# Two-layer decoder trunk on one core: four units of second-row products kept back ahead of an inner norm, and one more weight residual of the next stage issued early

## Chip, cores and metric

The kernel runs on 1 core of one Trainium2 chip. The metric is device time in microseconds (us); lower is better. The kernel before takes 2195.03 us, the median of 3 runs (2194.04 to 2196.49).

## What is computed

A trunk of two layers works on x, 256 rows (positions) of 2048 float32 values. Each layer has two sub-layers, a token mixer and a gated feed-forward with a short convolution, and each sub-layer ends in a LayerNorm:

```python
for i in range(DEPTH):                       # DEPTH = 2
    mod = c_act @ ada_w[i] + ada_b[i]        # 6 vectors of 2048 from the condition c
    sh1, sc1, g1, sh2, sc2, g2 = split(mod, 6)
    h = x * (1 + sc1) + sh1
    y = fox_attention(h, w_in, b_f, w_o) if i == 0 else swa_attention(h, pos, w_in, sinks, w_o)
    x = layer_norm(ALPHA * x + (1 + g1) * y, ln_mix_g[i], ln_mix_b[i])
    h = x * (1 + sc2) + sh2
    y = conv_ffn(h, w_up, conv_w, conv_b, w_down)
    x = layer_norm(ALPHA * x + (1 + g2) * y, ln_ffn_g[i], ln_ffn_b[i])
```

Everything is float32. A LayerNorm needs the mean and variance of a whole row of x, so all 2048 columns of a row have to be there before the next sub-layer's h can be formed from it. There are four norms: three inner ones, called A (after the mixer of layer 0, near 455 us), B (after the feed-forward of layer 0, near 1188 us) and C (after the mixer of layer 1, near 1451 us), and the last one at the end.

## The kernel before, in words

**Tiles.** The 256 rows are two halves of 128 (`NT` = 2): the first rows (t = 0) and the second rows (t = 1). TensorE multiplies in a reduced-precision format, so every operand is split into a high and a low part, and one product takes three matmuls: high by high, high by low, low by high. For weights the high part `wh` is a cast on ScalarE (line 254) and the low part, the residual `wl`, a subtraction on VectorE (line 265).

**Units.** `stream` (line 233) walks a block of 512 weight columns in units of 256 contraction rows. For each unit it issues a DMA (half of a 1 MB tile in pool `wp`, 6 buffers), the cast into `wh`, and puts a function `go` into the list `work`. `go` runs the unit's matmuls, steps the deferred generators (`run_post`), takes one of the `feeds`, and calls `tick`. The pool `hl` holds 4 pairs `wh`, `wl`. Three units are pending at a time (`settle(2)`).

**When a residual is issued.** `rest` (line 202) walks the work list from the item that is about to run and issues the residuals of the units that it meets until it has counted three units (two, if the item is no unit). Items put in with `then(fn, True)` are in the set `lone`: at the first of these the count is raised to two (lines 206 and 207). At a norm three lone items stand between the last unit of the stage and the first of the next: the deferred last `residual`, `flush`, and `between`. The units of the next stage are called u0', u1', u2', u3' here.

**The end of a stage.** The last column block (d = 3) before a norm uses `x_mm_end` (line 284) with n = 2 in the three inner norms: the last n units multiply for the first rows only; the second rows' products of these units are kept back and run together behind them. So the first rows' sums are complete some time before the second rows'. `residual` (line 534) then does for each half, on VectorE: `tmp = ps * gate` (line 537), `x += tmp` (539), `bn_stats` (544), `bn_aggr` (547), `+EPS` (549), and a power on GpSimd (550) that gives 1/sigma. For the first rows a further small operation, `nm` = -mu/sigma (line 543), is pinned behind the second rows' addition. The last norm of the kernel uses n = 8 with four units' pairs placed in the buffer `hpad` (`spares`, line 309).

**Between stages.** `between` (line 1068) lets TensorE do filler matmuls (`spin`), then `modulate` (485) runs two feeds ahead of the first unit: `normalise` (554; first rows on ScalarE, line 560, second rows on VectorE, line 562), transposes of x on TensorE (446), and the modulation into `hH` and `hL` (lines 456 to 458 for the first four blocks, 460, 464, 84 and 85 for the rest). The remaining six feeds go one per unit.

**What sets the order.** The instructions are traced in the order of the work list, and a list scheduler at build time may move an instruction ahead of earlier ones on its engine where it takes it to be ready sooner. `pin` puts an instruction behind the one traced just before it on its engine. `behind[0] = 2` (line 1077) pins the next two residuals after a norm.

**The condition vectors.** `mod` is computed on VectorE as a background task: 192 columns, each a 1 MB DMA into a `wp` buffer and one multiply-reduce (`wa`, line 364). `tick` adds `ada["rate"]` to a debt and runs one column when the debt reaches 1; after the scale vector of a sub-layer's second half the task is held until the next `between`.

Of the kernel before, what the change touches and what calls it, by code (L numbers as in the profile page):

```python
# [14 lines left out]
ALU = mybir.AluOpType  # L15
# [3 lines left out]
D = 2048  # L19
S = 256  # L20
NT = S // P
KC = D // P
# [14 lines left out]
WB = 512  # L37
# [4 lines left out]
def hybrid_trunk(ctx: ExitStack, tc: tile.TileContext, a: dict, out: bass.AP):  # L42
    nc = tc.nc
# [33 lines left out]
    def pin(ins, on=True):  # L77

        if on:
            tc.keep_in_program_order(ins)  # L80
# [47 lines left out]
    for j in range(D // WB):  # L128
        ps = bank("cb")
# [72 lines left out]
    def rest(*items):  # L202

        n = 0
        for f in items:
            if f in lone:
                n = max(n, 2)
            if f in residuals:
                residuals[f]()
                n += 1  # L210
            elif f in weights:
                n += 1
            if n > 2 - (items[0] not in weights):
                return
# [60 lines left out]
    def x_mm(ps, kc, h, l, stat, last, first=0, ts=range(NT), js=range(2)):  # L275

        for t in ts:
            for i in js:
                xh, xl = stat(kc + i, t)
                mm(ps[t], xh, h[:, i, :], start=kc + i == first)  # L280
                mm(ps[t], xh, l[:, i, :])
                mm(ps[t], xl, h[:, i, :], stop=kc + i == last)

    def x_mm_end(ps, stat, nk, n):

        kept = []

        def use(kc, h, l):
            end = kc >= nk - 2 * n
            x_mm(ps, kc, h, l, stat, nk - 1, ts=(0,) if end else range(NT))  # L290
            if end:
                kept.append((kc, h, l))
            if kc + 2 >= nk:
                for e in kept:
                    x_mm(ps, *e, stat, nk - 1, ts=(1,))

        return use
# [8 lines left out]
                mm(o, wh, hL[:, kc + i, :], skip_group_check=True)  # L306
                mm(o, wl, hH[:, kc + i, :], stop=kc + i == last, skip_group_check=True)

    def spares(nk):
        t = [hpad[:, 56 + i * 2 * WB:56 + (i + 1) * 2 * WB].rearrange("p (a f) -> p a f", a=2) for i in range(8)]  # L310
        return {nk - 16 + 2 * i: (t[2 * i], t[2 * i + 1]) for i in range(4)}

    def x_stationary(wsrc, col, k0, nk, stat, end=0):

        ps = x_banks()
        use = x_mm_end(ps, stat, nk, end) if end else lambda kc, h, l: x_mm(ps, kc, h, l, stat, nk - 1)
        stream(wsrc, k0, col, list(range(nk)), use, spares(nk) if end == 8 else {})
        return ps

    def w_stationary(wsrc, col):  # L320
# [213 lines left out]
    def residual(ps, d, gate, last):  # L534
        for t in range(NT):
            tmp = ttile()
            nc.vector.tensor_tensor(tmp, ps[t], gate[:, d * 512:(d + 1) * 512], op=ALU.mult)
            xs = x[:, t, d * 512:(d + 1) * 512]
            nc.vector.tensor_tensor(xs, xs, tmp, op=ALU.add)  # L539
            if last:  # L540
                if t == 1 and d == D // 512 - 1:
                    mu, rs, nm = moments[0]
                    pin(nc.vector.scalar_tensor_tensor(nm, mu, -1.0, rs, op0=ALU.mult, op1=ALU.mult))
                nc.vector.bn_stats(stats[:, t, d, :], xs)  # L544
                if d == D // 512 - 1:
                    mv = sp.tile([P, 2], F32, tag="mv", name="mv")
                    nc.vector.bn_aggr(mv, stats[:, t].rearrange("p a b -> p (a b)"))
                    rs = sp.tile([P, 2], F32, tag="rs", name="rs")
                    nc.vector.tensor_scalar_add(mv[:, 1:2], mv[:, 1:2], EPS)
                    nc.gpsimd.tensor_tensor(rs[:, 0:1], mv[:, 1:2], mhalf, op=ALU.pow)  # L550
                    moments[t] = (mv[:, 0:1], rs[:, 0:1], rs[:, 1:2])
            yield
# [101 lines left out]
    def out_proj(oT, full, w_o, l):  # L654
        def stat(kc, t):
            while kc not in full:
                step()
            return oT[kc][0][:, t * P:(t + 1) * P], oT[kc][1][:, t * P:(t + 1) * P]

        ps = {d: x_banks() for d in range(2)}  # L660

        def part(d, ks):
            use = x_mm_end(ps[d], stat, KC, 2) if d == D // WB - 1 else                 lambda kc, h, l_: x_mm(ps[d], kc, h, l_, stat, KC - 1)
            stream(w_o, 0, d * WB, ks, use)

        for i, ks in enumerate((range(0, 8), range(8, 12))):
            then(lambda i=i: ada.update(rate=(0.72, 0.43)[l]))
            for d in range(2):
                part(d, list(ks))
        then(lambda: (ada_need(l, 2), ada.update(rate=(0.72, 0.65)[l])))  # L670
        for d in range(D // WB):
            if d < 2:
                part(d, list(range(12, KC)))
            else:
                ps[d] = x_banks()
                part(d, list(range(KC)))
            then(lambda d=d: defer(residual(ps[d], d, gates[l, 2], True)), d == D // WB - 1)
        then(lambda: (flush(), ada.update(gate_free=True)), True)
# [320 lines left out]
    def conv_ffn(l):  # L999
        w_up, w_dn = a["ffn_w_up"][l], a["ffn_w_down"][l]  # L1000
        NB = DFF // WB
        cw = lambda j, f: ccol[:, l, j, f:f + 1]

        def conv(pf, f):
            u = tp.tile([P, S], F32, tag="u", bufs=3, name="u")
            nc.scalar.activation(u, pf, AF.Identity, bias=cw(CW, f), scale=cw(2, f))  # L1006
            nc.vector.scalar_tensor_tensor(u[:, 1:], pf[:, :S - 1], cw(1, f), u[:, 1:],  # L1007
                                           op0=ALU.mult, op1=ALU.add)
            nc.vector.scalar_tensor_tensor(u[:, 2:], pf[:, :S - 2], cw(0, f), u[:, 2:],  # L1009
                                           op0=ALU.mult, op1=ALU.add)  # L1010
            return u

        def evac(ps, f0, then):
            u = None
            for f in range(5):
                v = conv(ps[f // 2][:, f % 2, :], f0 + f) if f < 4 else None
                if u is not None:
                    then(f - 1, u)
                u = v
                yield  # L1020
                yield

# [12 lines left out]

        sbs = [(0, 6), (6, NB)]
        if l == 0:
            then(lambda: later([rotary()]))
        for si, (b0, b1) in enumerate(sbs):
            gT = []  # L1040
            then(lambda: ada.update(rate=(0.32, 0.2)[l]))
            for b in range(b0, b1):
                ps = w_stationary(w_up, b * WB)
                sil = [ttile("sil") for _ in range(2)]
                then(lambda ps=ps, b=b, sil=sil: defer(evac(ps, b * 4, silu(sil))))
                ps = w_stationary(w_up, DFF + b * WB)
                then(lambda ps=ps, b=b, sil=sil, gT=gT: defer(evac(ps, DFF // P + b * 4, gated(sil, gT))))

            def stat(kc, t, gT=gT):
                while kc >= len(gT):  # L1050
                    run_post()
                return gT[kc][:, 0, t * P:(t + 1) * P], gT[kc][:, 1, t * P:(t + 1) * P]

            def ready(si=si):
                if si == 0:
                    drain()
                ada_need(l, 5)
                ada["rate"] = (0.45, 0.2)[l]

            then(ready)  # L1060
            for d in range(D // WB):
                ps = x_stationary(w_dn, d * WB, b0 * 4, (b1 - b0) * 4, stat, (2, 8)[l] if si > 0 and d == D // WB - 1 else 0)
                then(lambda ps=ps, d=d, si=si: defer(residual(ps, d, gates[l, 5], si == len(sbs) - 1)),
                     si > 0 and d == D // WB - 1)
        then(lambda: (flush(), ada.update(gate_free=True)), True)


    def between(l, v, g, b, name, ll):

        ada_need(l, v)  # L1070
        ada_need(l, v + 1)
        place(60 if v else 32)
        o = bank("spin")
        ada["held"] = False
        spin(o, 3)
        modulate(*merged(l, v, g, b, ll), normalise, o)
        behind[0] = 2
        later([affine(name, ll, 0 if v else 7)])

    for l in range(DEPTH):  # L1080
# [60 lines left out]
```

## Time and profile before

| | before |
|---|---|
| median of 3 runs | 2195.03 us (2194.04 to 2196.49) |
| profiled execution, its own time | 2194.81 us |
| span in the profile | 2193.0 us |
| TensorE matmul (PE) busy | 2138.1 us, 97% |
| VectorE (DVE) busy | 1764.0 us, 80% |
| ScalarE (ACT) busy | 1161.5 us, 53% |
| bytes read from HBM | 594.18 MB, 272 GB/s over the span |
| granted TensorE clock, mean | 0.993 |

How to read what follows. A row of the timeline has the start and duration in us, the engine, the line of the kernel, the operation, the tile written and the tiles read, the count, and in brackets the idle time of the engine just before it with what ended it. A row of the windows view has the stretch, its length, and the busy time of each engine in it with the number of instructions, then the granted TensorE clock (1.00 is full speed), the DMA share and GB/s. PE is the matmul side of TensorE and PEld its weight loads; SPq is the queue that issues DMAs. A matmul's end is modelled, so starts are the better mark.

### The profile page before, as it was taken

Reading aid. Unit: us, or ns where it says so; the run is one execution under the profiler, and the core shown is the slowest. Engines: PE = TensorE matmul, PEld = TensorE weight load, DVE = VectorE, ACT = ScalarE, POOL = GpSimd, SP = SyncE. Lnnn points to the kernel's source line nnn. Section 1 sums busy time; section 2 is a strip of 40 time slices with the busy share of each in tenths; the row PEclk is TensorE's granted clock in tenths of the full one; section 3 lists DMA queues with packets and bytes.
Section 4 is the critical chain, followed back from the end, with each engine's and each line's share of the span. In section 5 each row is a group of like instructions: output and inputs, shape, how many; then the busy total and the mean of one; then the engine's idle time right before and its main releaser. Section 6 shows DMA issues by size and latency. Waiting matters only on the chain.

```text
span 2193.0 us, 36167 instructions
## 1 busy us (share of the span) xinstructions
PE 2138.1 (97%) x14694; PEld 1948.5 (89%) x14694; DVE 1764.0 (80%) x2412; ACT 1161.5 (53%) x1771; POOL 11.5 (1%) x34
## 2 busy tenths in 40 slices
PE   6999999899999999999999999999999999999997
PEld 6999887689999888999987877789999988999986
DVE  7988899989989888898998876679787655666765
ACT  4546566355575433555554577555556533555541
POOL 1000000000000000000000000000000000000000
PEclk9999999999999999999999999999999999999999
DMA  9998999958878898887998653458776555555552
GB/s 385 421 373 307 359 340 338 346 205 343 325 281 324 325 364 341 321 316 284 329 349 308 238 189 130 154 175 305 272 268 248 192 194 193 195 197 196 193 196 98
DMA packets 89657, 598.63 MB, mean 273 GB/s; under 512 B 10017, under 2 KB 12353, under 8 KB 21137
## 3 DMA queue, kind: packets, MB, share of 16 engines
q1 hardware_dynamic: 89312, 595.87, 73.5%
q8 instruction: 115, 1.88, 0.3%
q0 software_dynamic: 176, 0.44, 0.1%
q14 instruction: 54, 0.43, 0.1%
HBM read 594.18 MB, written 2.10 MB: 272 GB/s over the span
## 4 chain that ended last, share of the span: by engine, by line
PE 85%; DVE 9%; ACT 3%; issue 2%; DMA 2%; SPq 0%; POOL 0%; DVEq 0%; ACTq 0%; POOLq 0%
PE ws L75 46%; PE xs L75 35%; DVE wa L364 3%; DVE wl L265 3%; DMA w<-in_fox_w_in_dram 2%; ACT wh L254 1%; PE o L75 1%; PE T L640 1%; PE S L75 1%; PE sm L446 0%; DVE x L581 0%; ACT pr L613 0%; DVE x L582 0%; DVE x L539 0%; DVE stats L544 0%
## 5 line engine op out<-in xcount | busy, mean ns | idle before, releaser
L254 ACT CAST wh<-w 128x1024 fp32r<-128x1024 f32 x724 | 761.4, 1053 | 804.4 <-PE xs L75 372.1
L265 DVE TENSOR_TENSOR wl<-w,wh 128x1024 fp32r<-128x1024 f32 x724 | 879.4, 1221 | 349.3 <-ACT wh L254 346.0
L75 PE MATMUL ws<-hH,wh 128*128 128x256 f32 x6656 | 1144.6, 276 | 8.6 <-ACT hH L473 7.5
L75 PEld LDWEIGHTS ws<-hH,wh 128*128 128x128 f32 x6656 | 1007.7, 188 | 13.5 <-ACT hH L473 7.9
L75 PE MATMUL ws<-hH,wl 128*128 128x256 f32 x3328 | 914.8, 276 | 4.3 <-DVE wl L265 4.3
L75 PEld LDWEIGHTS ws<-hH,wl 128*128 128x128 f32 x3328 | 625.0, 188 | 5.7 <-DVE wl L265 5.5
L364 DVE CUSTOM_DVE_ANT_0 wa<-wa,cb,acol 128x2048 f32<-128x2048 f32 x192 | 449.4, 2343 | 0.2 <-DVE cb L134 0.2
L75 PE MATMUL xs<-wh,gT 128*128 128x512 f32 x1376 | 424.6, 389 | 0.0
L75 PEld LDWEIGHTS xs<-wh,gT 128*128 128x128 f32 x1376 | 258.3, 188 | 53.6
L75 PE MATMUL xs<-wl,gT 128*128 128x512 f32 x688 | 267.7, 389 | 0.0
L75 PE MATMUL xs<-wh,hH 128*128 128x512 f32 x704 | 237.2, 403 | 2.8 <-ACT wh L254 2.8
L75 PEld LDWEIGHTS xs<-wh,hH 128*128 128x128 f32 x704 | 132.6, 190 | 32.8 <-ACT wh L254 3.4
L75 PEld LDWEIGHTS xs<-wl,gT 128*128 128x128 f32 x688 | 129.2, 188 | 26.7
L75 PE MATMUL xs<-wl,hH 128*128 128x512 f32 x352 | 139.9, 398 | 2.8 <-DVE wl L265 2.8
L75 PE MATMUL xs<-wh,oT 128*128 128x512 f32 x384 | 128.7, 405 | 0.0
L1006 ACT ACTIVATE u<-ws,ccol 128x256 f32<-128x256 f32 x176 | 96.8, 562 | 58.6 <-PE ws L75 46.0
L1007 DVE SCALAR_TENSOR_TENSOR u<-ws,ccol,u 128x255 f32<-128x255 f32 x176 | 82.4, 477 | 12.2 <-ACT u L1006 12.2
L75 PEld LDWEIGHTS xs<-wh,oT 128*128 128x128 f32 x384 | 74.1, 194 | 16.8 <-ACT oT L84 0.6
L1009 DVE SCALAR_TENSOR_TENSOR u<-ws,ccol,u 128x254 f32<-128x254 f32 x176 | 83.2, 477 | 2.2
L75 PE MATMUL xs<-wl,oT 128*128 128x512 f32 x192 | 77.4, 404 | 6.8 <-DVE wl L265 6.8
L75 PEld LDWEIGHTS xs<-wl,hH 128*128 128x128 f32 x352 | 66.7, 190 | 16.6 <-DVE wl L265 3.5
L613 ACT ACTIVATE pr<-pr,nm 128x128 f32<-128x128 f32 x96 | 43.2, 452 | 25.5 <-DVE nm L609 25.4
(195 smaller groups left out, 1103.3 us busy)
## 6 DMA issues: line engine op xcount, KB each, us to landing
wa<-in_ada_w_dram SPq DMA_DIRECT2D x192, 1024.0 KB, 7.1
w<-in_ffn_w_up_dram SPq DMA_DIRECT2D x176, 1024.0 KB, 5.7
w<-in_ffn_w_down_dram SPq DMA_DIRECT2D x88, 1024.0 KB, 5.0
w<-in_fox_w_in_dram SPq DMA_DIRECT2D x60, 512.0 KB, 8.6
w<-in_swa_w_in_dram SPq DMA_DIRECT2D x20, 1024.0 KB, 6.3
w<-in_fox_w_in_dram SPq DMA_DIRECT2D x18, 1024.0 KB, 7.3
w<-in_fox_w_o_dram SPq DMA_DIRECT2D x16, 1024.0 KB, 7.4
w<-in_swa_w_o_dram SPq DMA_DIRECT2D x16, 1024.0 KB, 4.7
```

The costliest lines, as they stand in the source:

```text
L75: return nc.tensor.matmul(o, lhsT, rhs, start=start, stop=stop, **kw)
L254: pin(nc.scalar.copy(h, w), False)
L265: pin(nc.vector.tensor_tensor(l, w, f32(h), op=ALU.subtract), behind[0] > 0)
L364: return nc.vector.tensor_tensor_reduce(w, w, cb, 1.0, acol[:, l, v * KC + k:v * KC + k + 1], ALU.mult, ALU.add, cv[:, k:k + 1])
L613: nc.scalar.activation(pr[:, b:e], pr[:, b:e], AF.Exp, bias=nm[:, r:r + 1], scale=-1.0, accum_out=ss[:, r:r + 1])
L640: nc.tensor.transpose(tps[:, b * P:(b + 1) * P], pr[:, b * P:(b + 1) * P], ident)
L1006: nc.scalar.activation(u, pf, AF.Identity, bias=cw(CW, f), scale=cw(2, f))
L1007: nc.vector.scalar_tensor_tensor(u[:, 1:], pf[:, :S - 1], cw(1, f), u[:, 1:], op0=ALU.mult, op1=ALU.add)
L1009: nc.vector.scalar_tensor_tensor(u[:, 2:], pf[:, :S - 2], cw(0, f), u[:, 2:], op0=ALU.mult, op1=ALU.add)
```

## The change

It has these parts:

1. `out_proj` (norms A and C) and the feed-forward of layer 0 (norm B) keep back the second rows' products of four units instead of two. Three of the four units' `wh`, `wl` pairs are placed in parts of `hpad` that are free then (`spares`, now with a second layout), so they don't hold buffers of `hl`. The four pairs of the last norm's layout are moved by 24 elements.
2. `rest` no longer raises its count at lone items, so the residual of u1' is issued along with that of u0', ahead of the norm. `behind[0] = 2` is gone: no residual is pinned any more.
3. In the last column block, the second rows' first operation in `residual` (line 537) is pinned behind the operation traced before it, the first rows' `+EPS` (line 549).
4. In the last column block before a feed-forward's norm the rate of the background task is set to 0; `between`'s caller or the next stage sets it again, as before.

```diff
         for f in items:
-            if f in lone:
-                n = max(n, 2)
             if f in residuals:
...
-    def spares(nk):
-        t = [hpad[:, 56 + i * 2 * WB:56 + (i + 1) * 2 * WB].rearrange("p (a f) -> p a f", a=2) for i in range(8)]
-        return {nk - 16 + 2 * i: (t[2 * i], t[2 * i + 1]) for i in range(4)}
+    def spares(nk, n):
+        at = lambda o: hpad[:, o:o + 2 * WB].rearrange("p (a f) -> p a f", a=2)
+        if n == 8:
+            return {nk - 16 + 2 * i: (at(32 + i * 4 * WB), at(32 + (2 * i + 1) * 2 * WB)) for i in range(4)}
+        return {nk - 8 + 2 * i: (at(32 + i * 2 * WB), at(60 + (8 + 2 * i) * WB)) for i in range(3)}
...
-        stream(wsrc, k0, col, list(range(nk)), use, spares(nk) if end == 8 else {})
+        stream(wsrc, k0, col, list(range(nk)), use, spares(nk, end) if end else {})
...
-            nc.vector.tensor_tensor(tmp, ps[t], gate[:, d * 512:(d + 1) * 512], op=ALU.mult)
+            pin(nc.vector.tensor_tensor(tmp, ps[t], gate[:, d * 512:(d + 1) * 512], op=ALU.mult),
+                last and t == 1 and d == D // 512 - 1)
...
-            use = x_mm_end(ps[d], stat, KC, 2) if d == D // WB - 1 else ...
-            stream(w_o, 0, d * WB, ks, use)
+            if d == D // WB - 1:
+                stream(w_o, 0, d * WB, ks, x_mm_end(ps[d], stat, KC, 4), spares(KC, 4))
+            else:
+                stream(w_o, 0, d * WB, ks, lambda kc, h, l_: x_mm(ps[d], kc, h, l_, stat, KC - 1))
...
-                ps = x_stationary(..., (2, 8)[l] if si > 0 and d == D // WB - 1 else 0)
+                if si > 0 and d == D // WB - 1:
+                    then(lambda: ada.update(rate=0.0))
+                ps = x_stationary(..., (4, 8)[l] if si > 0 and d == D // WB - 1 else 0)
...
         modulate(*merged(l, v, g, b, ll), normalise, o)
-        behind[0] = 2
         later([affine(name, ll, 0 if v else 7)])
```

More of the change, by code (lines that the diff above doesn't have):

```diff
@@ L662, in part @@
         def part(d, ks):
-            use = x_mm_end(ps[d], stat, KC, 2) if d == D // WB - 1 else                 lambda kc, h, l_: x_mm(ps[d], kc, h, l_, stat, KC - 1)
-            stream(w_o, 0, d * WB, ks, use)
+            if d == D // WB - 1:
+                stream(w_o, 0, d * WB, ks, x_mm_end(ps[d], stat, KC, 4), spares(KC, 4))
+            else:
+                stream(w_o, 0, d * WB, ks, lambda kc, h, l_: x_mm(ps[d], kc, h, l_, stat, KC - 1))
         for i, ks in enumerate((range(0, 8), range(8, 12))):
@@ L1061, in conv_ffn @@
             for d in range(D // WB):
-                ps = x_stationary(w_dn, d * WB, b0 * 4, (b1 - b0) * 4, stat, (2, 8)[l] if si > 0 and d == D // WB - 1 else 0)
+                if si > 0 and d == D // WB - 1:
+                    then(lambda: ada.update(rate=0.0))
+                ps = x_stationary(w_dn, d * WB, b0 * 4, (b1 - b0) * 4, stat, (4, 8)[l] if si > 0 and d == D // WB - 1 else 0)
                 then(lambda ps=ps, d=d, si=si: defer(residual(ps, d, gates[l, 5], si == len(sbs) - 1)),
```

## The prediction, made before the changed kernel was run

> **What bounds the kernel now.** I read the page's busy shares and its chain first, then asked for the stretches around the three inner norms, then read the timeline engine by engine there.
>
> ```profile
> span 2193.0 us, 36167 instructions
> PE 2138.1 (97%) x14694; PEld 1948.5 (89%) x14694; DVE 1764.0 (80%) x2412; ACT 1161.5 (53%) x1771; POOL 11.5 (1%) x34
> PE 85%; DVE 9%; ACT 3%; issue 2%; DMA 2%; SPq 0%; POOL 0%; DVEq 0%; ACTq 0%; POOLq 0%
> ```
>
> TensorE is busy for all but 55 us and carries 85% of the chain that ends last. So the number of matmuls sets nearly all of the time, the change leaves that number alone, and it can only win or lose time where TensorE stands idle or works slowly. The norms are such places. The windows view, from the start of the last kept-back product to the start of the first product of the next stage, for A, B and C:
>
> ```profile
> 455.19:461.01 5.82, 4.47 (x20) 2.64 (x19) 4.85 (x13) 4.47 (x8) 1.12 (x2) 1.00 0.00 0
> 1187.47:1196.13 8.66, 6.08 (x20) 3.86 (x19) 7.14 (x19) 5.58 (x10) 1.09 (x2) 0.80 0.32 130
> 1450.70:1456.59 5.89, 4.48 (x21) 2.65 (x19) 4.93 (x13) 4.51 (x8) 1.10 (x2) 1.00 0.00 0
> ```
>
> A and C take 5.82 and 5.89 us; B takes 8.66, which is 2.81 more than their mean of 5.85, and its granted clock is 0.80 where theirs is 1.00. The same instructions stand in all three; so B has something that A and C haven't.
>
> **What sets the gap at A and C.** VectorE and ScalarE at A:
>
> ```profile
> 452.82 0.69 DVE L537 TENSOR_TENSOR t<-xs,gate 128x512 f32<-128x512 f32 x1 [3.21 <-PE xs L75]
> ...
> 455.30 0.15 DVE L549 TENSOR_SCALAR mv<-mv 128x1 f32<-128x1 f32 x1
> 455.62 0.69 DVE L537 TENSOR_TENSOR t<-xs,gate 128x512 f32<-128x512 f32 x1 [0.17 <-PE xs L75]
> ...
> 456.96 0.15 DVE L543 SCALAR_TENSOR_TENSOR rs<-mv,rs 128x1 f32<-128x1 f32 x1
> ...
> 458.92 1.92 DVE L562 TENSOR_SCALAR x<-x,mv,rs 128x512 f32<-128x512 f32 x4 [0.67 <-POOL rs L550]
> ...
> 461.66 0.75 DVE L458 TENSOR_TENSOR hH<-t,hH 128x256 fp32r<-128x256 f32 x2
> ...
> 463.90 2.35 DVE L265 TENSOR_TENSOR wl<-w,wh 128x1024 fp32r<-128x1024 f32 x2
> ```
>
> ```profile
> 457.14 2.23 ACT L560 ACTIVATE x<-x,rs 128x512 f32<-128x512 f32 x3 [0.48 <-DVE rs L543]
> ```
>
> Both multiplications of line 537 are released by TensorE. They lie 455.62 - 452.82 = 2.80 us apart: that is what the kept products of two units take. The first rows' work takes 455.30 + 0.15 - 452.82 = 2.63 us, so it is over 0.17 us before the second rows' sums come. From there the second rows' chain runs alone: 458.92 - 455.62 = 3.30 us to their normalisation. C shows the same:
>
> ```profile
> 1451.13 0.69 DVE L537 TENSOR_TENSOR t<-xs,gate 128x512 f32<-128x512 f32 x1
> ...
> 1454.49 1.92 DVE L562 TENSOR_SCALAR x<-x,mv,rs 128x512 f32<-128x512 f32 x4 [0.73 <-POOL rs L550]
> ```
>
> Here it is 3.36 us. So keeping back four units in place of two makes the second rows' products last 5.60 us instead of 2.80, moves the first rows' work 2.80 us earlier, and shortens nothing at A and C: the second rows' sums come when they came, and `nm` (456.96), which releases ScalarE's normalisation of the first rows, stays pinned behind the second rows' addition. Worth 0 there. Without this edit the pin of part 3 would have only 0.17 us to spare; with it, 2.97 us.
>
> **What is different at B.**
>
> ```profile
> 1182.66 2.34 DVE L364 CUSTOM_DVE_ANT_0 wa<-wa,cb,acol 128x2048 f32<-128x2048 f32 x1
> ...
> 1185.91 0.69 DVE L539 TENSOR_TENSOR x<-x,t 128x512 f32<-128x512 f32 x1
> 1187.91 0.69 DVE L537 TENSOR_TENSOR t<-xs,gate 128x512 f32<-128x512 f32 x1 [1.31 <-PE xs L75]
> 1188.52 0.68 DVE L544 BATCH_NORM_STATS2 stats<-x 128x6 f32<-128x512 f32 x1
> ...
> 1192.12 1.92 DVE L562 TENSOR_SCALAR x<-x,mv,rs 128x512 f32<-128x512 f32 x4 [0.66 <-POOL rs L550]
> ...
> 1194.85 0.75 DVE L458 TENSOR_TENSOR hH<-t,hH 128x256 fp32r<-128x256 f32 x2
> ```
>
> The order was changed here: the second rows' multiplication stands ahead of the first rows' `bn_stats`, waits 1.31 us for TensorE, and only then, in the second rows' chain, do the first rows' statistics run. That chain takes 1192.12 - 1187.91 = 4.21 us, 0.88 more than the mean 3.33 of A and C. TensorE meanwhile:
>
> ```profile
> 1187.47 0.40 PE L75 MATMUL xs<-wh,gT 128*128 128x512 f32 x1
> ...
> 1192.29 2.18 PE L446 MATMUL sm<-ident,x 128*128 128x128 f32 x8 [2.49 <-ACT x L560]
> 1194.27 2.32 PE L75 MATMUL spin<-mask,ident 128*128 128x384 f32 x4
> 1196.13 0.69 PE L75 MATMUL xs<-wh,hH 128*128 128x512 f32 x1
> ```
>
> ```profile
> 459.52 0.66 PE L446 MATMUL sm<-ident,x 128*128 128x128 f32 x4 [0.86 <-DVE x L562]
> 460.01 1.46 PE L75 MATMUL spin<-mask,ident 128*128 128x384 f32 x4
> 461.01 0.69 PE L75 MATMUL ws<-hH,wh 128*128 128x256 f32 x2
> ```
>
> At B all eight transposes come after a wait of 2.49 us and take 1.98 us from start to start; at A four take 0.49, so eight would take 0.98. The four spins take 1.86 us at B and 1.00 at A. That is 1.00 + 0.86 = 1.86 us of slow clock, which fits the granted clock: 0.20 of 8.66 us is 1.73. And 0.88 + 1.86 = 2.74 accounts for the 2.81.
>
> **Part by part.**
>
> *The pin, the four units and the stopped background task at B.* The pin puts the first rows' statistics ahead of the second rows' multiplication. What waits behind that on VectorE is the rest of the second rows' chain, and behind it ScalarE through `nm`; the wait costs nothing as long as the first rows are done. Their sums come at 1187.91 - 5.60 = 1182.31, their work would end at 1184.94, 2.97 us early. The column at 1182.66 would have stood in the way by up to 2.34 us; setting the rate to 0 takes it away. So B should look like A: a gain of 2.81 us at most. VectorE's own part may not shrink as far: the first low parts (line 458, the first of two) are there at 1194.85 + 0.38 = 1195.23, and 0.88 earlier is 1194.35, while the first product would start at 1196.13 - 2.81 = 1193.32 and its third matmul, two spacings of 0.23 (2.80 us for 12) later, needs them. It could lose 0.6 us there. Bounds 0.88 (if the clock is lost all the same) and 2.81; I take 2.4, nearer the rows of A and C.
>
> By the Trainium skill, page "TensorE: Matmul & The Clock Gate", section "What's actually happening", the clock halves after an idle window of about 3.4 us and comes back after one as long that is busy. The trace agrees with the second half only: 1.73 us lost is about 3.4 us at half speed, but the idle wait before it was 2.49 us.
>
> *Residuals.* `wl` of u1' moves ahead of the norm, out of the pair at 463.90 (2.35 us for two). Ahead of it VectorE idles for 3.21 us (452.82 row), and in the new order for 2.97 us behind the first rows' work; without such cover 1.18 us would be added. What it relieves is the VectorE queue behind the norm. Where TensorE waits there:
>
> ```profile
> 476.00:520.00 44.00, 42.00 (x362) 41.17 (x361) 44.00 (x77) 24.42 (x34) 0.00 (x0) 1.00 0.79 293
> 1476.00:1520.00 44.00, 43.76 (x385) 43.55 (x384) 43.90 (x64) 25.62 (x34) 0.00 (x0) 1.00 0.80 294
> ```
>
> ```profile
> 509.94 1.22 DVE L265 TENSOR_TENSOR wl<-w,wh 128x1024 fp32r<-128x1024 f32 x1
> 511.21 0.38 PE L75 MATMUL ws<-hH,wl 128*128 128x256 f32 x1 [1.92 <-DVE wl L265]
> ```
>
> Behind A VectorE is busy for all of 44 us and TensorE loses 1.92 us in one wait for a residual; behind C TensorE loses 0.24. One residual less in that queue is 1.18 us, two (u2' is no longer pinned, and its buffers are free early) 2.35. Bounds at A 0 and 1.92, I take 1.5 (between the two sizes of relief); at C 0.1. Next in line then is TensorE itself.
>
> *Moved work.* At a rate of 0.45 the ten units of the last block ran 4 or 5 columns; call it 5. Each is a DMA, a multiply-reduce and a short read:
>
> ```profile
> L364 DVE CUSTOM_DVE_ANT_0 wa<-wa,cb,acol x192: 2326/2344/2353, 10.9 to 1667.7; 128x2048 f32<-128x2048 f32 x192
> wa<-in_ada_w_dram SPq DMA_DIRECT2D x192, 1024.0 KB, 7.1
> 1262.00:1342.00 80.00, 77.98 (x463) 59.72 (x462) 57.09 (x187) 60.44 (x157) 0.00 (x0) 0.98 0.47 172
> PE S L75 <- DVE qL L85: 0.8, 1, 0.8
> ```
>
> They run at the end of the row of columns in the sliding-window stage, roughly from 1270 to 1340 at its rates of 0.3 to 0.33 a unit. That is 5 x 2.34 = 11.7 us on a VectorE that is idle for 22.9 of 80 us, and five 1 MB transfers on DMA engines at 0.47. Hidden: I take 0. Without cover one column in front of `qL`, on which TensorE waited 0.8 us, costs up to 2.34 us; below nothing it can't go, since nothing waits for these columns before norm C. On the SP queue five `wa` issues leave the stretch before B and join this one; the weights of the next stage only come sooner. The casts of units in `hpad` wait for no buffer, and ScalarE is 53% busy. For layer 1 the rate of 0 and the moved `hpad` pairs of the last norm change no instruction: 0.
>
> Sum: 2.4 + 1.5 + 0.1 = 4.0 us less. On the profiled execution's own 2194.81 us (span 2193.0) that is 2190.8; it stands 0.22 below the median of 2195.03, so the median becomes 2191.0. A measurement of this kernel can tell about 0.2%, 4.4 us, from no change: this forecast is 0.18%.
>
> **Rivals.**
>
> *All at the upper end:* 2.8 + 1.9 + 0.2 = 4.9, so 2190.1. For it: A and C are a model of B in every row. Against: the low parts above.
>
> *The moved columns collide* with the attention of the second layer: 2.3 us given back, 2193.3. For it: the 0.8 us wait on `qL`. Against: 22.9 us of idle time.
>
> *The clock at B stays slow.* The first rows' normalisation is still behind `nm`, so TensorE still waits, though less; if the slow stretch comes anyway B gains 0.9, the sum is 2.5, the time 2192.5. For it: a gap remains. Against: A and C have it with a clock of 1.00. The page's rule gives this result another way: 2.49 us being too short a window, something other than the wait would have slowed B's clock.
>
> *The freed residuals get into the chain.* Unpinned, `wl` of u2' or u3' could be put between the second rows' multiplication and their normalisation, as `bn_stats` was at B. One at a norm makes the chain 1.18 us longer, more than B's 0.88, so the clock would go as it went at B, another 1.86: A and C lose 3.04 each, B has its 2.81 less 3.04, and the relief of 1.6 stays. That is 6.08 + 0.23 - 1.6 = 4.7 slower, 2199.7. It decides from one residual at each of the three norms on; at one norm alone the sum is still below nothing. Against: with four kept units VectorE has 2.97 idle us ahead of that chain, and a list scheduler fills the earlier gap first.
>
> **How the numbers follow.** The forecast has 0.60, and since its terms may each be half a microsecond off (2189.9 to 2191.8) 0.28 of that lies beyond 0.2%. Upper end 0.12, collision 0.13, slow clock 0.08, chain 0.07. Faster: 0.28 + 0.12 = 0.40. Same: 0.32 + 0.13 + 0.08 = 0.53. Slower: 0.07. The range goes from the upper end less the runs' scatter of 1.2 us, 2188.9, to the collision and as much, 2194.5; it leaves out the chain and the tails.
>
> **What would show it.** Right: at B the gap falls to about 6 us with a clock of 1.00, `bn_stats` of the first rows stands ahead of the second rows' multiplication, that chain takes 3.3 us at all three norms, A's and C's gaps stay at 5.8 to 5.9, no wait for `wl` of over 1 us behind A, and no `wa` between 1160 and 1188. Wrong: a gap at A or C that is shorter by more than half a microsecond, a `wl` inside the chain, or new waits on `qL` past 1266.

## The result and the profile after

The changed kernel takes 2199.81 us, the median of 22 runs (2195.28 to 2202.22), beside 2195.18 us for the kernel before in 22 runs of the same session (2192.83 to 2197.11). The ratio is 1.0017 with an interval of 1.0010 to 1.0024: slower, by 4.6 us between the medians, where 4.0 us faster was forecast. The 22 times fall into two groups, ten from 2195.28 to 2197.80 and twelve from 2199.77 to 2202.22; the times of the kernel before form one. The profiled execution of after, 2196.16 us, belongs to the lower group; one of the upper group was profiled later (experiment 3).

The page of after, its span, busy shares and chain:

```profile
span 2194.3 us, 36164 instructions
PE 2137.4 (97%) x14694; PEld 1947.5 (89%) x14694; DVE 1763.7 (80%) x2412; ACT 1160.7 (53%) x1771; POOL 11.5 (1%) x34
PE 84%; DVE 10%; ACT 3%; DMA 2%; issue 1%; SPq 0%; POOL 0%; DVEq 0%; ACTq 0%; POOLq 0%
```

The number of matmuls is the same, VectorE and ScalarE do the same amount of work, and the span is 1.3 us longer. A difference of this size isn't to be found in totals. The windows view of after, from the start of the last kept-back product to the first product of the next stage, at A, B and C:

```profile
454.41:461.31 6.90, 4.47 (x20) 2.65 (x19) 5.59 (x12) 5.10 (x8) 0.55 (x1) 1.00 0.42 148
1187.61:1194.51 6.90, 4.48 (x21) 2.65 (x19) 5.60 (x12) 5.10 (x8) 0.55 (x1) 1.00 0.40 141
1449.65:1458.03 8.38, 5.89 (x20) 3.54 (x19) 6.86 (x15) 5.91 (x9) 0.55 (x1) 0.82 0.31 125
```

B fell from 8.66 to 6.90, 1.76 of the 2.81 us that the forecast held possible there. But A rose from 5.82 to 6.90 and C from 5.89 to 8.38. Cut at these gaps, the two profiled spans differ so: -0.78 up to A, +1.08 in A, -0.16 from A to B, -1.76 in B, +0.57 from B to C, +2.49 in C, -0.14 to the end; together +1.3. The timeline of VectorE in after shows what came in at A:

```profile
449.27 0.69 DVE L537 TENSOR_TENSOR t<-xs,gate 128x512 f32<-128x512 f32 x1 [4.49 <-PE xs L75]
449.88 1.22 DVE L263 TENSOR_TENSOR wl<-w,wh 128x1024 fp32r<-128x1024 f32 x1
451.01 0.68 DVE L540 TENSOR_TENSOR x<-x,t 128x512 f32<-128x512 f32 x1
...
452.76 0.15 DVE L550 TENSOR_SCALAR mv<-mv 128x1 f32<-128x1 f32 x1
454.84 0.69 DVE L537 TENSOR_TENSOR t<-xs,gate 128x512 f32<-128x512 f32 x1 [1.92 <-PE xs L75]
455.56 0.69 DVE L540 TENSOR_TENSOR x<-x,t 128x512 f32<-128x512 f32 x1
456.17 0.15 DVE L544 SCALAR_TENSOR_TENSOR rs<-mv,rs 128x1 f32<-128x1 f32 x1
456.24 1.22 DVE L263 TENSOR_TENSOR wl<-w,wh 128x1024 fp32r<-128x1024 f32 x1
457.38 0.69 DVE L545 BATCH_NORM_STATS2 stats<-x 128x6 f32<-128x512 f32 x1
...
459.22 1.46 DVE L563 TENSOR_SCALAR x<-x,mv,rs 128x512 f32<-128x512 f32 x3 [0.67 <-POOL rs L551]
```

Two unpinned residuals stand here. The one at 449.88, for u2', runs in the first rows' time, 1.92 idle us ahead of the second rows' multiplication: the longer time of the kept products hides it. The one at 456.24, for u3', stands in the second rows' chain, between `nm` and `bn_stats`. That chain takes 459.22 - 454.84 = 4.38 us here, where it took 3.30. ScalarE's timeline tells why this residual couldn't come earlier:

```profile
454.84 1.04 ACT L252 CAST wh<-w 128x1024 fp32r<-128x1024 f32 x1 [10.05 <-PE xs L75]
```

The cast of u3' waits for the last kept-back product and starts in the same hundredth of a microsecond as the second rows' multiplication. Its residual can be ready only inside the chain. B has it at the same place:

```profile
1188.04 0.69 DVE L537 TENSOR_TENSOR t<-xs,gate 128x512 f32<-128x512 f32 x1 [2.91 <-PE xs L75]
...
1189.44 1.22 DVE L263 TENSOR_TENSOR wl<-w,wh 128x1024 fp32r<-128x1024 f32 x1
...
1192.41 1.46 DVE L563 TENSOR_SCALAR x<-x,mv,rs 128x512 f32<-128x512 f32 x3 [0.66 <-POOL rs L551]
```

The chain is 4.37 us at B and, from the like rows, 4.44 us at C. TensorE's side of it in after, the second rows' transposes at A, B and C, and the filler matmuls at C:

```profile
459.82 0.66 PE L446 MATMUL sm<-ident,x 128*128 128x128 f32 x4 [1.94 <-DVE x L563]
...
1193.02 0.66 PE L446 MATMUL sm<-ident,x 128*128 128x128 f32 x4 [1.93 <-DVE x L563]
...
1455.13 1.12 PE L446 MATMUL sm<-ident,x 128*128 128x128 f32 x4 [2.00 <-DVE x L563]
1456.04 2.64 PE L75 MATMUL spin<-mask,ident 128*128 128x384 f32 x4
```

The wait ahead of these transposes was 0.86 us at A before; now it is 1.93 to 2.00 at all three. A and B still ran at a clock of 1.00 in this execution, C did not: the same four transposes took 1.12 us in place of 0.66 and the four filler matmuls 2.64 in place of 1.46. So the added residual costs 1.08 us of waiting at each norm, and at C another 1.4 us of slow clock.

### The profile page after: what moved, and what is told of

It reads as the page before. It is cut to its first block, busy times and chain, and to the rows that moved or that the text cites. A ratio compares the mean times of both kernels' runs of the same rounds, so it can differ in the third digit from the quotient of the medians.

```text
span 2194.3 us, 36164 instructions
## 1 busy us (share of the span) xinstructions
PE 2137.4 (97%) x14694; PEld 1947.5 (89%) x14694; DVE 1763.7 (80%) x2412; ACT 1160.7 (53%) x1771; POOL 11.5 (1%) x34
## 4 chain that ended last, share of the span: by engine, by line
PE 84%; DVE 10%; ACT 3%; DMA 2%; issue 1%; SPq 0%; POOL 0%; DVEq 0%; ACTq 0%; POOLq 0%
PE ws L75 46%; PE xs L75 35%; DVE wa L364 3%; DVE wl L263 3%; DMA w<-in_fox_w_in_dram 2%; PE o L75 1%; ACT wh L252 1%; PE T L641 1%; PE S L75 1%; PE sm L446 0%; DVE x L582 0%; ACT pr L614 0%; DVE x L583 0%; DVE x L540 0%; PE sm L75 0%
## 5 line engine op out<-in xcount | busy, mean ns | idle before, releaser
L252 ACT CAST wh<-w 128x1024 fp32r<-128x1024 f32 x715 | 751.7, 1053 | 804.4 <-PE xs L75 384.8
L263 DVE TENSOR_TENSOR wl<-w,wh 128x1024 fp32r<-128x1024 f32 x715 | 868.4, 1220 | 332.4 <-ACT wh L252 328.9
L75 PE MATMUL xs<-wh,gT 128*128 128x512 f32 x1352 | 417.5, 389 | 0.0
L75 PEld LDWEIGHTS xs<-wh,gT 128*128 128x128 f32 x1352 | 253.8, 188 | 52.3
L75 PE MATMUL xs<-wl,gT 128*128 128x512 f32 x676 | 263.0, 389 | 0.0
L75 PE MATMUL xs<-wh,oT 128*128 128x512 f32 x352 | 118.5, 405 | 0.0
L75 PEld LDWEIGHTS xs<-wh,oT 128*128 128x128 f32 x352 | 67.8, 193 | 15.3 <-ACT oT L84 0.4
L75 PE MATMUL xs<-wl,oT 128*128 128x512 f32 x176 | 70.9, 404 | 6.8 <-DVE wl L263 6.8
L537 DVE TENSOR_TENSOR t<-xs,gate 128x512 f32<-128x512 f32 x48 | 31.7, 684 | 35.7 <-PE xs L75 35.7
```

Of the source, the lines that this page charges most:

```text
L75: return nc.tensor.matmul(o, lhsT, rhs, start=start, stop=stop, **kw)
L252: pin(nc.scalar.copy(h, w), False)
L263: pin(nc.vector.tensor_tensor(l, w, f32(h), op=ALU.subtract), behind[0] > 0)
L537: pin(nc.vector.tensor_tensor(tmp, ps[t], gate[:, d * 512:(d + 1) * 512], op=ALU.mult), last and t == 1 and d == D // 512 - 1)
```

## The experiments

The theory is that the pin of part 3 (or the kept products of part 1) cures B, and that part 2 spoils all three norms by letting the residual of u3' into the chain. Its rivals: the changed clock or the moved columns of part 4 make the loss; the four kept units cost something of their own; or any VectorE work in that place would do, the residual being nothing special.

The gaps of all kernels, by the windows view, in us with the granted clock:

| kernel | A | B | C |
|---|---|---|---|
| before | 5.82 (1.00) | 8.66 (0.80) | 5.89 (1.00) |
| after, lower group | 6.90 (1.00) | 6.90 (1.00) | 8.38 (0.82) |
| after, upper group (3) | 6.90 (1.00) | 7.77 (0.89) | 8.38 (0.80) |
| residuals pinned again (1) | 5.82 (1.00) | 5.82 (1.00) | 5.89 (1.00) |
| pin of part 3 alone (2) | 5.82 (1.00) | 5.82 (1.00) | 5.89 (1.00) |
| only u3' pinned (4) | 5.82 (1.00) | 5.82 (1.00) | 5.89 (1.00) |
| part 1 alone (5) | 5.82 (1.00) | 5.83 (1.00) | 5.89 (1.00) |
| part 2 alone (6) | 8.30 (0.93) | 10.47 (0.77) | 7.86 (1.00) |
| after, two units kept (7) | 8.31 (0.93) | 9.16 (0.81) | 9.27 (0.74) |
| padded chain (8) | 7.23 (0.98) | 8.49 (0.83) | 8.57 (0.79) |
| (1) without part 4 (9) | 5.82 (1.00) | 5.83 (1.00) | 5.89 (1.00) |
| (1), normalisation pinned (10) | 5.82 (1.00) | 5.82 (1.00) | 5.89 (1.00) |

**1. The residuals pinned again.** After, with the one line of part 2 that pinned them put back:

```diff
         modulate(*merged(l, v, g, b, ll), normalise, o)
+        behind[0] = 2
```

> The changed kernel with one line put back: the next two residuals after a norm are pinned again (behind[0] = 2). Theory (the freed residual of u3' stands in the second rows' chain at every norm and lets the clock drop in some executions): the chain from the second rows' multiplication to their normalisation falls from 4.4 to 3.3 us at A, B and C, the gaps from 6.9, 6.9 and 8.4 us to 5.8 to 5.9 at a clock of 1.00, and the time to 2191.5 (2196.16 less 1.1, 1.1 and 2.5), in one mode. Rival 1 (the four kept units and their pairs in hpad cost the time): the chain is 3.3 but the time stays at 2196 or above. Rival 2 (the moved columns cost it): the time falls by less than 3 us and the stretch from B to C stays 2 us or more over that of before.

It takes 2191.40 us (2190.00 to 2192.93, 11 runs) beside 2194.91 for before; the ratio is 0.9984 (0.9975 to 0.9993). Its windows:

```profile
455.92:461.74 5.82, 4.47 (x20) 2.65 (x19) 4.62 (x11) 4.39 (x7) 0.55 (x1) 1.00 0.00 0
1188.25:1194.07 5.82, 4.48 (x21) 2.65 (x19) 4.62 (x11) 4.39 (x7) 0.55 (x1) 1.00 0.01 3
1447.94:1453.83 5.89, 4.49 (x21) 2.66 (x19) 4.63 (x11) 4.39 (x7) 0.55 (x1) 1.00 0.00 0
```

VectorE has 11 instructions and about 4.6 us of work in each, where after has 12 and 5.6 at A and B: the residual is gone, and with it the whole loss. B is at A's length, 2.84 us shorter than before. Against the first profile of after, the three gaps are 1.08 + 1.08 + 2.49 = 4.65 us shorter, close to the 4.4 us between the two spans (2194.3 and 2189.9). The remaining stretches differ too, and mostly by the clock: it is 0.93 in after and 0.86 here from 430 to 454 us, and 0.98 in after and 1.00 here from 1222 to 1300.

**2. The pin of part 3 alone**, in the kernel before:

```diff
-            nc.vector.tensor_tensor(tmp, ps[t], gate[:, d * 512:(d + 1) * 512], op=ALU.mult)
+            pin(nc.vector.tensor_tensor(tmp, ps[t], gate[:, d * 512:(d + 1) * 512], op=ALU.mult),
+                last and t == 1 and d == D // 512 - 1)
```

> The kernel before with the pin of the second rows' multiplication alone (part 3). Theory: at B the first rows' statistics go ahead, the chain falls from 4.2 to 3.3 us, the gap from 8.7 to about 5.9 at a clock of 1.00; A and C as before; time 2192.4. Rival (at B it is the background column, not the order, that makes the gap): the gap at B stays over 8 us and the time at 2195.

2191.88 us (2189.97 to 2193.78), ratio 0.9986 (0.9978 to 0.9995). At B the first rows' `bn_stats` starts at 1186.06, ahead of the second rows' multiplication at 1187.33, and the normalisation comes at 1190.63, a chain of 3.30 us. One pin wins all that the change could win at B; two kept units give it room enough.

**3. After once more**, unchanged, to see how its two groups differ.

> The changed kernel once more, for a profile of another execution. Theory: times in two groups, near 2196.4 and near 2200 to 2202; a profile of the upper group shows granted clocks under 1.00 at two or three of the norms, one of the lower group at one; the chains are 4.4 us in either. Rival (the upper group is slow somewhere else, as in the attention): the norms' gaps are the same as in the first profile.

2200.64 us (2195.54 to 2201.93, 11 runs), ratio 1.0022 (1.0013 to 1.0031). Two of the 11 lie under 2196, one at 2198.41, the rest from 2199.96 up. The profiled execution took 2200.64. Its windows behind A, at B and behind B:

```profile
478.00:522.00 44.00, 41.98 (x352) 41.55 (x351) 43.83 (x76) 24.04 (x33) 0.00 (x0) 0.96 0.80 296
1190.54:1198.31 7.77, 5.35 (x20) 3.01 (x19) 6.46 (x14) 5.91 (x9) 0.55 (x1) 0.89 0.40 137
1198.31:1222.00 23.69, 23.69 (x113) 19.14 (x112) 18.02 (x26) 13.16 (x19) 0.00 (x0) 0.96 0.28 94
```

It is the same program with the residuals at the same places. What differs is where the clock was lost: here also at B (0.89 of 7.77 us) and in two stretches behind the norms, 0.04 of 44 us = 1.76 and 0.04 of 23.69 = 0.95. Against the first profile of after the span is 4.5 longer: 1.63 from A to B, 0.87 in B, 0.86 from B to C, -0.16 behind C, and 1.30 ahead of A. The last is clock as well: near 437 us both executions wait 4.25 us for a residual, and from 430 to 454 us the clock is 0.86 here and 0.93 there, 0.07 of 24 us = 1.68. The kernel before has 0.86 too, so it is not the change that does it. By these two profiles, the upper group is the lower one with the clock lost in more places.

**4. Only the residual of u3' pinned**, u2' free:

```diff
-                pin(nc.vector.tensor_tensor(l, w, f32(h), op=ALU.subtract), behind[0] > 0)
+                pin(nc.vector.tensor_tensor(l, w, f32(h), op=ALU.subtract), behind[0] == 1)
...
+        behind[0] = 2
```

> The changed kernel with the residual of u3' alone pinned behind the norm; that of u2' stays free. Theory (it is the one of u3', whose cast ends just as the second rows' chain begins, that does the harm; that of u2' runs while VectorE waits for the second rows): gaps of 5.8 to 5.9 us at all three norms and a time of 2191.4 within 1. Second question, whether relief of VectorE's queue behind A is worth something: by the prediction the wait of 1.9 us for a residual near 510 us would shrink; by the runs so far it stays, since VectorE then waits for TensorE's transposes instead. Rival (u2' does the harm): 2196 or more.

2191.16 us (2190.49 to 2194.04), ratio 0.9986 (0.9977 to 0.9995). VectorE's timeline at A, and TensorE's wait behind it:

```profile
451.25 1.22 DVE L263 TENSOR_TENSOR wl<-w,wh 128x1024 fp32r<-128x1024 f32 x1
...
456.21 0.69 DVE L537 TENSOR_TENSOR t<-xs,gate 128x512 f32<-128x512 f32 x1 [1.92 <-PE xs L75]
```

```profile
511.28 0.38 PE L75 MATMUL ws<-hH,wl 128*128 128x256 f32 x1 [1.86 <-DVE wl L263]
```

The residual of u2' is in the first rows' time as in after, and all gaps are at their short length: the loss is u3' alone. And though u2' is ahead here, the wait near 511 us stays at 1.86 (1.84 in experiment 1, 1.92 before).

**5. Part 1 alone**: four units kept, their pairs in `hpad`, with `lone`, `behind`, no pin and the old rate as in the kernel before.

```diff
-            pin(nc.vector.tensor_tensor(tmp, ps[t], gate[:, d * 512:(d + 1) * 512], op=ALU.mult),
-                last and t == 1 and d == D // 512 - 1)
+            nc.vector.tensor_tensor(tmp, ps[t], gate[:, d * 512:(d + 1) * 512], op=ALU.mult)
```

> The kernel before with part 1 alone: four kept units with their pairs in hpad; residuals pinned as before, the second rows not pinned, the background task not stopped. Theory (the four units cost nothing themselves): A and C stay at 5.8 to 5.9 us; at B the first rows have 2.8 us more, so their statistics go ahead of the second rows even without the pin and the gap falls to 5.8; time 2192. Rival (the pairs in hpad or the longer run of second-row products cost time): 2196 or more, with A and C unchanged and the loss outside the gaps.

2191.41 us (2190.20 to 2194.45), ratio 0.9985 (0.9976 to 0.9993). The four units cost nothing of their own; they cure B without the pin, since the first rows' `bn_stats` starts at 1185.02 at B, ahead of the second rows' multiplication at 1186.96. Parts 1 and 3 are two cures for one fault.

**6. Part 2 alone**, in the kernel before:

```diff
-            if f in lone:
-                n = max(n, 2)
...
-        behind[0] = 2
```

> The kernel before with part 2 alone: no count of lone items, no pinned residuals; two kept units, no pin of the second rows. Theory (freed residuals get into the second rows' chain): two of them reach it at each norm, since the first rows' work leaves 0.17 us free ahead of it; the first operation of the chain starts about 1 us late or the chain is 1.1 us longer for each, so the gaps are 7 to 10 us at A and C and over 9 at B, with clocks under 1.00; time 2200 to 2206. Rival (the freed residuals relieve the queue behind the norm, and only together with four kept units do they harm): 2194 or less.

2200.25 us (2199.26 to 2204.50, 10 runs) beside 2195.44, ratio 1.0024 (1.0015 to 1.0034). VectorE at A, and TensorE's wait there:

```profile
455.94 1.23 DVE L263 TENSOR_TENSOR wl<-w,wh 128x1024 fp32r<-128x1024 f32 x1
457.08 0.68 DVE L535 TENSOR_TENSOR t<-xs,gate 128x512 f32<-128x512 f32 x1
457.69 1.22 DVE L263 TENSOR_TENSOR wl<-w,wh 128x1024 fp32r<-128x1024 f32 x1
```

```profile
460.47 0.66 PE L444 MATMUL sm<-ident,x 128*128 128x128 f32 x4 [2.39 <-ACT x L558]
```

Here both are on the path: one delays the second rows' multiplication, the other stands behind it, ahead of the addition and of `nm`. So here it is the first rows' transposes that wait, 2.39 us, because ScalarE's normalisation waits for `nm`. A is 2.48 us longer than before, B 1.81, C 1.97.

**7. After with two units kept** at the inner norms:

```diff
-        stream(wsrc, k0, col, list(range(nk)), use, spares(nk, end) if end else {})
+        stream(wsrc, k0, col, list(range(nk)), use, spares(nk, end) if end == 8 else {})
...
-                stream(w_o, 0, d * WB, ks, x_mm_end(ps[d], stat, KC, 4), spares(KC, 4))
+                stream(w_o, 0, d * WB, ks, x_mm_end(ps[d], stat, KC, 2))
...
-                ps = x_stationary(..., (4, 8)[l] if ...)
+                ps = x_stationary(..., (2, 8)[l] if ...)
```

> The changed kernel with two kept units in place of four, pairs in the pool as before; its parts 2, 3 and 4 stay. Theory (with two units there is no idle time ahead of the second rows in which a freed residual could run): two residuals delay the chain at each norm instead of one, 2.2 us in place of 1.1, and the clock goes at nearly every norm: gaps 8 to 10 us, time 2201 to 2206. Rival (it is the four kept units that cost the time): 2192 to 2196.

2201.53 us (2200.96 to 2202.66, 6 runs), ratio 1.0029 (1.0018 to 1.0041). At B one `wl` starts at 1191.23 ahead of the multiplication at 1192.37, and one at 1192.97 behind it. This is what the four units do in after: with them the residual of u2' has time of VectorE to hide in (1.92 idle us are still left at A), without them it too is on the path, and the gaps grow to 8.31, 9.16 and 9.27.

**8. The chain padded**: experiment 2 with two dead VectorE multiplications of 128x512 pinned in the second rows' chain, behind `nm` and ahead of `bn_stats`, at the last norm too.

```diff
+                    idle = f32(gtile("idle")).rearrange("p a b -> p (a b)")
+                    for _ in range(2):
+                        pin(nc.vector.tensor_tensor(idle, cb[:, :512], cb[:, 512:1024], op=ALU.mult))
-                nc.vector.bn_stats(stats[:, t, d, :], xs)
+                pin(nc.vector.bn_stats(stats[:, t, d, :], xs), t == 1 and d == D // 512 - 1)
```

> The kernel before with the pin of the second rows' multiplication (which took 2191.9 us) and, in the second rows' chain behind nm, two added VectorE multiplications of 512 columns each that nobody reads, pinned there (about 1.2 us in all); it measures the price of time in the chain by itself, without residuals, four units or moved columns. Theory: the chain grows by 1.2 us at each of the three norms, the wait of TensorE between the first and second rows' transposes from 0.9 to about 2.0, the gaps to 7.0 us with a full clock and to 7.8 to 8.9 with a lost one; the last norm adds about 1.2 too; time 2196 to 2202, with a wider scatter than the pin alone. Rival (only the clock of a residual's neighbours matters, and 1.2 us of chain costs 1.2 us each): 2196.5 to 2197 in one narrow group.

2202.10 us (2200.59 to 2204.53, 5 runs) beside 2195.21, ratio 1.0032 (1.0019 to 1.0045). VectorE, then TensorE at A, then the window behind A's transposes:

```profile
458.06 1.41 DVE L547 TENSOR_TENSOR idle<-cb 128x512 f32<-128x512 f32 x2
...
461.23 1.46 DVE L566 TENSOR_SCALAR x<-x,mv,rs 128x512 f32<-128x512 f32 x3 [0.67 <-POOL rs L554]
```

```profile
461.83 0.66 PE L446 MATMUL sm<-ident,x 128*128 128x128 f32 x4 [2.13 <-DVE x L566]
```

```profile
463.46:469.00 5.54, 5.54 (x35) 5.24 (x34) 5.17 (x10) 1.85 (x4) 0.00 (x0) 0.72 0.16 41
```

No residual is moved here, and 1.41 us of other work in the same place do what the residual's 1.22 did, and more: waits of 2.12 to 2.19 us, gaps of 7.23 to 8.57, and a clock of 0.72 behind A (0.28 of 5.54 is 1.6 us), of 0.83 in B and 0.79 in C. So the place and the length count, whatever the work is for. Compared with experiment 2 it costs 10.2 us between the medians. The last norm has a small part in this: from the start of the last product to the end of the span it is 2202.7 - 2189.37 = 13.33 us, where experiment 2 has 2189.6 - 2177.52 = 12.08.

**9. Experiment 1 without part 4**, so that the background columns run as in the kernel before:

```diff
-                if si > 0 and d == D // WB - 1:
-                    then(lambda: ada.update(rate=0.0))
+        behind[0] = 2
```

> The changed kernel with the residuals pinned again (which took 2191.4 us) and the background task not stopped ahead of the feed-forward's norm (part 4 undone). Theory: at B a column stands ahead of the first rows' multiplication, but they have 2.97 us to spare, so the gap stays 5.8; from B to C it is 0 to 0.7 us shorter; time 2190.7 to 2191.9. Rival (the column delays the second rows): the gap at B is over 6.5 us and the time over 2192.5.

2192.80 us (2190.05 to 2193.72), ratio 0.9985 (0.9976 to 0.9993), which can't be told from experiment 1, though it lies above the 2191.9 expected. A column starts at 1182.43 and takes 2.35 us, ahead of the first rows' multiplication at 1184.70; the second rows' comes at 1187.43, and B's gap is 5.83 all the same. So stopping the task wins nothing at B. What moving the columns costs elsewhere is less than these times can tell.

**10. The second rows' normalisation pinned** at its place in experiment 1's kernel, an attempt to bring the first block's modulation and the residuals behind it into a tighter order:

```diff
-                nc.vector.tensor_scalar(xs, xs, mu, rs, op0=ALU.subtract, op1=ALU.mult)
+                pin(nc.vector.tensor_scalar(xs, xs, mu, rs, op0=ALU.subtract, op1=ALU.mult), d > 0)
+        behind[0] = 2
```

> As the first kernel of this call, and the second rows' normalisation of the column blocks 1 to 3 is pinned at its place too, so that VectorE modulates the first blocks before it. Theory (the gap's end hangs on VectorE's queue behind the chain): the first low parts come 1.4 us after the normalisation sooner at best, the gaps shrink by 0.3 to 0.7 us each, time 1 to 2 us under the first kernel's, about 2190. Rival (TensorE waits for ScalarE's high parts and the spins anyway): the same time as the first kernel's within 0.5.

2197.30 us (2196.70 to 2198.90), ratio 1.0010 (1.0002 to 1.0019), 5.9 us more than experiment 1, where 1 to 2 us less was expected. The gaps don't change; VectorE is earlier at the modulation and then waits for ScalarE, as its row and the window behind A show:

```profile
461.15 1.00 DVE L457 TENSOR_SCALAR t<-sm,G,B 128x256 f32<-128x256 f32 x2 [1.02 <-ACT hH L456]
```

```profile
477.00:521.00 44.00, 41.27 (x340) 40.27 (x339) 44.00 (x76) 22.84 (x31) 0.00 (x0) 0.96 0.77 283
```

From A's first product to B's last kept-back one it is 729.57 us where experiment 1 has 726.51, and from C's first product to the end 738.33 where it has 736.07. The clock row accounts for 0.04 of 44 us, 1.76. TensorE also idles longer: 2.73 us of this window, where the like one of experiment 1 (477 to 521) has 2.14, and 1.29 of the first 15.13 us behind C, where experiment 1 has 0.24 of 16.17. That is 3.4 of the 5.3 us; the rest stays open.

## Why the prediction was wrong

**The pin, the four units and B: right.** Forecast 2.4 with bounds of 0.88 and 2.81; without the residual in the way it is 2.84, at the upper bound: the low parts of line 458, which were to cost up to 0.6, didn't hold the first product back. That each of the two edits is enough by itself was not seen: "Without this edit the pin of part 3 would have only 0.17 us to spare" counted 0.17 us as little, and experiment 2 shows that they suffice; experiment 5 shows that part 1 suffices without the pin.

**The freed residuals, priced at nothing in the second rows' chain, so that "A's and C's gaps stay at 5.8 to 5.9": wrong, and this is the step that failed.** Instead each norm has one residual of 1.22 us in the chain, and each gap is 1.08 us longer than in experiment 1, which takes it out, with another 1.41 us of slow clock at C. The fault isn't in "Worth 0 there", which is said of the four kept units and holds (5.82 and 5.89 in experiment 5). It is in the part on the residuals, where the sum counts them only as relief and takes the cover for granted ("Ahead of it VectorE idles for 3.21 us", said of u1'). The prediction looked for room on VectorE and never asked when the residual's own input is there. ScalarE's timeline of the kernel before would have told it:

```profile
455.62 1.04 ACT L254 CAST wh<-w 128x1024 fp32r<-128x1024 f32 x1 [0.35 <-PE xs L75]
```

This cast starts with the second rows' multiplication (455.62 too), released by the last kept-back product, as its counterpart in after at 454.84. Its residual becomes ready within the second rows' chain and not before it. Experiments 1 and 4 show the cost by taking it out, 6 and 7 by adding to it, 8 by imitating it.

**The rival that came true was named, and set at 0.07.** "A list scheduler fills the earlier gap first" is true of u2' and no argument for u3', which can't be put into the earlier gap. The prediction's own sign of this rival, "a `wl` inside the chain", is the row at 456.24. Its price was near: 1.18 us of wait at each norm were priced, 1.08 measured. It took the clock as lost at all norms, 1.86 each; measured, 1.4 at C in one execution, and at C, at B in part and in two stretches behind the norms in the other. Its 2199.7 lies beside the median of 2199.81, but partly by chance: the relief of 1.6 in that sum did not come, and the clock was lost elsewhere than it said.

**Residual relief, 1.5 at A: wrong too.** It is the second largest term of the sum, and it came out at 0.06: the wait of 1.92 us behind A became 1.86. The windows behind A, of the kernel before and of after:

```profile
461.01:476.00 14.99, 14.99 (x130) 14.81 (x129) 14.90 (x21) 9.21 (x14) 0.00 (x0) 1.00 0.55 202
```

```profile
461.31:476.00 14.69, 14.69 (x126) 14.38 (x125) 12.26 (x19) 8.72 (x13) 0.00 (x0) 1.00 0.22 74
```

VectorE has three residuals less to do here (and one step of the normalisation more) and is busy for 2.64 us less, but it doesn't run ahead: in its timeline 2.42 us of idle time come in instead, 2.18 of them before the modulations of line 464, which wait for TensorE's transposes, and 0.24 for a cast. The transposes are fed one block per unit, so TensorE's own pace sets them. At 473.90 VectorE starts the same background column that it started at 474.05 before, and from there the queue up to 510 us is the same. The relief was worked out from the length of the queue at the place of the wait; 40 us ahead of it the queue was not what bound. The 0.1 forecast at C is too small to be told.

**Moved columns, 0: right** within what can be told, for no more than about half a microsecond is in sight. From B to C after takes 0.57 us more than before. Experiment 1, which moves the same columns, takes 0.70 less, but that is the clock and no proof: from 1222 to 1300 us it is 1.00 there and 0.98 in both before and after, 0.02 of 78 us = 1.56. Among the executions that show 0.98 there and 1.00 in the rest of the stretch, after and experiment 7 take 255.14 and 254.95 us from B to C with the columns moved, and before and experiments 2, 5 and 9 take 254.55 to 254.77 without.

**The clock.** In twenty gaps at A, B and C with short waits (A and C of before, all three of experiments 1, 2, 4, 5, 9 and 10), it stayed at 1.00; at B of before it was lost after 2.49 us. That a wait between these would cost the clock in some executions and not in others was not in the forecast; the two profiles of after, one of each group, differ mostly by it.

## What to carry to other kernels

When a scheduler is given more freedom, take each operation that is set free and ask when its inputs are there: if they come at the start of a dependent chain, the operation will be ready inside the chain, and idle time ahead of it is no cover. A queue that is full at the place of a wait is relieved by earlier work only if nothing between is bound by something else. And measure the parts of a change alone: here part 3 alone takes 3.0 us off the kernel before and part 1 alone 4.0, while part 2 alone adds 4.8.

## What the runs showed of the hardware

TensorE's clock was lost after waits of about 2 us, but not after all of them. With the same program and waits of 1.93 to 2.00 us at A, B and C, one execution of after kept it at A and B and lost it at C (0.82); the other kept it at A, lost part of it at B (0.89) and lost it at C (0.80). A wait of 2.39 us at A of experiment 6 was followed by a loss (0.93), one of 2.46 us at its C by none. The loss could come later than the gap: in experiment 8 the gap at A shows 0.98, and the 5.54 us behind it 0.72. It isn't special to the norms, where a wait of 0.49 us and four transposes come just before the longer wait. In the second execution of after, a wait of 1.85 us for a residual at 512 us, between products at full speed, was followed by a clock of 0.59 from 514 to 518 us, while in the kernel before 1.92 us at the same place cost nothing (1.00). Nor is 2 us a lower limit. In the sliding-window attention of layer 1, near 1282 us, TensorE in after waits 1.10 and then 0.62 us and shows 0.79 from 1282 to 1286 us; experiment 1 waits just as long there and shows 1.00.

The Trainium skill, page "TensorE: Matmul & The Clock Gate", section "What's actually happening", has the idle window at about 3.4 us and calls it free-running. The length disagrees with these rows, where 2.49 us (B of before) and 1.85 us of waiting were enough; that a window tied to nothing in the program would make the outcome differ between executions fits the two profiles of after. No run here shows the window itself, so why one execution loses the clock and another doesn't stays open. Open too is why the kernel before, which pins the residuals of u1' and u2' alone, kept that of u3' out of the chain.
